# Attention of a float32 encoder layer: probabilities and values as whole float32 operands instead of split float16 halves, with the maxima chain reordered

## The chip, the core and the metric

One core of a Trainium2 chip runs the whole layer. The metric is device time in microseconds (us) of one execution, as the median of several. TensorE's clock is granted at one of two levels, 1.2 or 2.4 GHz; the profile gives it as 0.5 or 1.0 of full speed.

## What is computed

A one-layer encoder runs over two sequences, a prompt of 512 tokens and a sample of 2048 tokens, with model width 1024. Inputs, weights and outputs are float32. The layer normalises, projects, mixes with windowed means and with attention, projects back, and ends with a convolutional feed-forward part of width 2816. The change lies in the attention (8 heads, query and key width 96, value width 64):

```python
def attend(q_blk):
    s = jnp.einsum('bqhd,bkhd->bhqk', q_blk, k_full).astype(jnp.float32) * scale
    p = jax.nn.softmax(s, axis=-1).astype(v.dtype)
    return jnp.einsum('bhqk,bkhd->bqhd', p, v)
```

## The kernel before

The kernel has three stages. The first (to about 352 us) makes queries, keys and values in chunks of 256 tokens; queries and keys go through DRAM, values stay in SBUF in the tile `V`. The second (352 to about 1275 us) is the attention. The third (the rest) is the output projection and the feed-forward part.

To keep float32 accuracy with float16 products, an operand is *split*: a high half (the value rounded to float16) and a low half (what the rounding left). A product then needs three half-products, high by high, high by low and low by high (`THREE`); low by low is dropped. `V` holds per head 64 low columns, 64 high columns and a column of ones, so that one product with 129 moving columns gives low, high and the sum of the probabilities at once.

The attention runs in *units* in a hand-written order: 16 units of the prompt (256 queries by 4 key tiles of 128, two PSUM banks of scores) and 128 units of the sample (128 queries by 16 key tiles, four banks). The steps of a unit, by function:

- `st_scores`: a bank of scores, 12 products of 128 columns on TensorE (PE).
- `st_max`, `st_fold`: the maximum over a bank's four tiles on VectorE (DVE), one reduction for each of four banks into `mx4`, then the fold of the four maxima (128 x 512 elements) into `mx`.
- `st_T`, `st_redT`, `st_rep`: a transpose of `mx` on PE, its row maximum on DVE with two small operations that cut it into two parts (`p3`), a transpose back on PE, and a copy to `mr` on ScalarE (ACT).
- `st_r1`: four products that subtract the maximum from the score banks.
- `st_exp`: the exponential, one ACT operation a bank, into `pf` (float32).
- `st_hi`, `st_lo`: `pf` split into `ph` (one bank by ACT, the other three by DVE casts) and `pl` (GpSimd, POOL, four subtractions).
- `st_pv`: for each key tile a product of `ph` with 129 columns of `V` and one of `pl` with 65.
- `st_out`, `st_out2`: a copy of the result out of PSUM, the sum of the two halves (POOL), the division by the sum of probabilities (DVE), and a store once in four units.

The order is a string of letters, one turn of it for each unit `i`; each letter emits a step, and every engine runs its instructions in that order:

```python
r=lambda i: some(st_r1, i, range(4)),
L=lambda i: some(st_scores, i + 1, [3]),
a=lambda i: some(st_scores, i + 2, [0]),
M=lambda i: some(st_max, i + 1, [3]),
N=lambda i: run(st_fold, i + 1),
LAG = 2
PARTS = [0, 10, 16]
ORDER = "r e0 A L M N P o e1 a T d f l1 b R i c h l0 l2 l3 x y z q"
```

`A` and `P` are the two parts of `st_pv` of unit `i - LAG`, `b` and `c` score banks 1 and 2 of unit `i + 2`, `x y z` the maxima of banks 0 to 2 of that unit, `T d R` the transpose, row maximum and transpose back of unit `i + 1`. Score banks rotate through seven PSUM banks, so `L` needs the bank that the first exponential of the same turn frees, `a` that of the second, `b` and `c` the next two. One further PSUM bank (`psX`) holds the results of `st_pv` and the two transposes. Between turns, `prep_w_out` prepares the output weights, one small piece at a time; one piece is a POOL reduction over all partitions whose result DVE reads in the next piece.

Of the kernel before, what the change touches and what calls it, by code (L numbers as in the profile page):

```python
# [38 lines left out]
LN_SHIFT = math.log(2.0 ** 14)  # L39
SCORE_SCALE = 1.0 / math.sqrt(QKD)  # L40
VW = 130
# [7 lines left out]
def encoder(ctx, tc, ins, outs, seq_names=("x_prompt", "x_sample")):  # L49
# [27 lines left out]
    ln_shift = small([P, 1], "ln_shift")  # L77
    dve.memset(ln_shift, LN_SHIFT)
    act.activation(small([P, 1], "warm"), ln_shift, AF.Square)
# [103 lines left out]
    V = vpool.tile([P, NTOK // P, H, VW], F16, name="V")  # L183
    pool.memset(V[:, :, :, 128:130], 1.0)

# [28 lines left out]
    with tp("wA", 1) as wA, tp("pA", 2) as pA, tc.manual_schedule():  # L214
# [605 lines left out]
    def prep_w_out(raw):  # L820
# [20 lines left out]
        yield  # L841
# [51 lines left out]
    with tp("pB", 2) as pB, tp("psX", 1, "right", space=PSUM) as psX, \  # L893
# [49 lines left out]
        def st_max(i, b):  # L943
            u = units[i]
            w = u["w"]
            t0, t1 = u["banks"][b]
            st = u["st"][b]
            if t1 - t0 == 4:
                if b == 0:
                    u["mx4"] = pB.tile([P, 4, P], F32, name=f"mx4_{i}", tag="mx4")  # L950
                dve.tensor_reduce(u["mx4"][:, b, :], st.rearrange("p (t q) -> p q t", q=w), axis=AX.X, op=ALU.max)  # L951
            elif b:
                for t in range(2):
                    dve.tensor_tensor(out=u["mx"][:, :w], in0=st[:, t * w:(t + 1) * w], in1=u["mx"][:, :w], op=ALU.max)
            else:
                u["mx"] = pB.tile([P, 256], F32, name=f"mx_{i}", tag="mx")
                dve.tensor_reduce(u["mx"][:, :w], st[:, :(t1 - t0) * w].rearrange("p (t q) -> p q t", q=w), axis=AX.X,
                                  op=ALU.max)

        def st_fold(i):  # L960

            u = units[i]
            if len(u["banks"]) == 4:
                u["mx"] = pB.tile([P, 256], F32, name=f"mx_{i}", tag="mx")
                dve.tensor_reduce(u["mx"][:, 0:P], u["mx4"].rearrange("p b q -> p q b"), axis=AX.X, op=ALU.max)

        def side_tile(i):

            if ("x", i) not in state:
                state["x", i] = psX.tile([P, 512], F32, name=f"x_{i}", tag="x")  # L970
            return state["x", i]

        def st_T(i):
            u = units[i]
            xp = side_tile(i - 1)
            old = units[i - 1 - LAG]["nq"] if i > LAG else 1
            u["alone"] = u["nq"] > 1 or old > 1
            u["mrp"] = xp[:, 512 - u["w"]:] if u["alone"] else xp[:, 129:129 + P]
            xp = u["xp"] = xp[:, 512 - u["w"]:]
            for j in range(u["nq"]):  # L980
                pe.matmul(xp[:, j * P:(j + 1) * P], u["mx"][:, j * P:(j + 1) * P], ident, is_transpose=True,
                          start=u["alone"], stop=True, skip_group_check=True)

        def st_redT(i):
# [4 lines left out]
            dve.tensor_reduce(m, u["xp"][:, :nq * P].rearrange("p (j k) -> p j k", j=nq), axis=AX.X, op=ALU.max)  # L989
# [8 lines left out]
        def st_rep(i):  # L998
# [3 lines left out]
            for j in range(nq):  # L1002
                pe.matmul(u["mrp"][:, j * P:(j + 1) * P], p3[:, j].rearrange("p a b -> p (a b)"), ident,  # L1003
                          is_transpose=True, start=u["alone"], stop=True, skip_group_check=True)
# [18 lines left out]
        def st_exp(i, b):  # L1023
            u = units[i]
            if b == 0:
                u["pf"] = pB.tile([P, 2048], F32, name=f"pf_{i}", tag="pf")
# [4 lines left out]
        def st_hi(i, b):  # L1031
            u = units[i]
            if "ph" not in u:
                u["ph"] = pB.tile([P, 2048], F16, name=f"ph_{i}", tag="ph", bufs=3)
                u["pl"] = pB.tile([P, 2048], F16, name=f"pl_{i}", tag="pl", bufs=3)
            c = cols(u, b)
            if b == 2 and len(u["banks"]) == 4:
                c = slice(c.start, cols(u, 3).stop)
            if b in (1, 2):
                dve.tensor_copy(u["ph"][:, c], u["pf"][:, c])  # L1040
            elif b == 0:
                act.activation(u["ph"][:, c], u["pf"][:, c], AF.Copy)

        def st_lo(i, b):
            u = units[i]
            c = cols(u, b)
            pool.tensor_tensor(out=u["pl"][:, c], in0=u["pf"][:, c], in1=u["ph"][:, c], op=ALU.subtract)  # L1047

        def st_pv(i, part):
            u = units[i]  # L1050
            s, h, nq, nkt, w = u["s"], u["h"], u["nq"], u["nkt"], u["w"]
            if part == 0:
                op = side_tile(i + LAG) if units[min(i + LAG + 1, NU - 1)]["nq"] == 1 else bank(f"op_{i}")
                u["op"] = op[:, :2 * 129].rearrange("p (j c) -> p j c", j=2)
# [4 lines left out]
            parts = PARTS  # L1059
            for j, t in jobs[parts[part] * n // 16:parts[part + 1] * n // 16]:  # L1060
                c0 = t * w + j * P
                pe.matmul(op[:, j, 0:129], u["ph"][:, c0:c0 + P], V[:, k0 + t, h, 0:129], start=t == 0, stop=False)  # L1062
                pe.matmul(op[:, j, 64:129], u["pl"][:, c0:c0 + P], V[:, k0 + t, h, 64:129], start=False,  # L1063
                          stop=t == nkt - 1)

        def st_out(i):
# [7 lines left out]
            tt = state[key]  # L1074
            act.activation(tt[:, qi % 4:qi % 4 + nq, 0:129], op[:, 0:nq, 0:129], AF.Copy)  # L1075
            if (qi + nq) % 4 == 0 or (qi + nq) * P == s["S"]:
                n = qi % 4 + nq
                pool.tensor_tensor(out=tt[:, :n, 64:128], in0=tt[:, :n, 64:128], in1=tt[:, :n, 0:64], op=ALU.add)

        def st_out2(i):  # L1080
# [6 lines left out]
            if (qi + nq) % 4 == 0 or (qi + nq) * P == s["S"]:  # L1087
                n = qi % 4 + nq
                ri = pB.tile([P, 4], F32, name=f"ri_{i}", tag="ri")
                dve.reciprocal(ri[:, :n], tt[:, :n, 128])  # L1090
# [5 lines left out]
                dve.tensor_tensor(out=ot[:, :n, b0:b0 + 64], in0=tt[:, :n, 64:128],  # L1096
# [8 lines left out]
        LAG = 2  # L1105
        PARTS = [0, 10, 16]
# [12 lines left out]
        def some(fn, k, bs):  # L1119
            if 0 <= k < NU:  # L1120
                for b in bs:
# [6 lines left out]
            e0=lambda i: some(st_exp, i, range(3)),  # L1128
            e1=lambda i: some(st_exp, i, [3]),
            A=lambda i: run(st_pv, i - LAG, 0),  # L1130
            P=lambda i: run(st_pv, i - LAG, 1),
            
# [6 lines left out]
            v=lambda i: some(st_max, i + 3, [0]),  # L1139
            w=lambda i: some(st_max, i + 3, [1]),  # L1140
# [4 lines left out]
            N=lambda i: run(st_fold, i + 1),  # L1145
            f=lambda i: some(st_hi, i, [1]),
            h=lambda i: some(st_hi, i, [0]),
            i=lambda i: some(st_hi, i, [2]),
            l0=lambda i: some(st_lo, i, [0]),
            l1=lambda i: some(st_lo, i, [1]),  # L1150
            l2=lambda i: some(st_lo, i, [2]),
            l3=lambda i: some(st_lo, i, [3]),
# [5 lines left out]
        START = ["a b x y", "a b T d t x u y R", "r e T d t R x y u f l1 h l0",  # L1158
                 "r e T d t R x y u f l1 h l0", "r e T d A P R x y f l1 h l0 o q"]
        ORDER2 = "r e T d a b x R f l1 y h A P q o l0 c z"  # L1160
        ORDER = "r e0 A L M N P o e1 a T d f l1 b R i c h l0 l2 l3 x y z q"
        for i in range(-2, NU):
            whole = units[min(max(i, 0) + 1, NU - 1)]["nq"] == 1
            for x in (START[i + 2] if i + 2 < len(START) else ORDER if whole else ORDER2).split():
# [9 lines left out]
        for i in range(NU, NU + LAG):  # L1174
            for part in range(2):
                run(st_pv, i - LAG, part)
            run(st_out2, i - LAG - 1)
            run(st_out, i - LAG)
            m = i - NU
            if m == 1:  # L1180
# [3 lines left out]
            if m == LAG - 1:  # L1184
# [3 lines left out]
            for t, m in todo[:4]:  # L1188
                c_mm2(t, m)
# [532 lines left out]
```

## Time and profile before

| | us |
|---|---|
| median of 3 runs (3246.03 to 3251.99) | 3248.72 |
| the profiled execution, its own time | 3256.74 |
| its span | 3254.9 |
| PE busy in the span | 3044.8 |
| DVE busy | 2161.2 |
| ACT busy | 1400.4 |
| POOL busy | 875.7 |

Busy time over the whole span says little here: the third stage is 60% of the span and has nothing to do with the change. Read the stage by itself, with the busy time of each engine in a stretch of it, then the waits in that stretch, then one unit instruction by instruction. A time line gives start and duration in us; where it merges several instructions into one line, the duration runs from the first start to the last end. The end of a product is modelled, so what a product costs PE is read from the distance between two starts.

### The profile page before, as it was taken

The numbers are of one execution on the slowest core, as the hardware profiler recorded it, in microseconds if no ns is written. First come the engines' busy times: TensorE is split into PE (matmuls) and PEld (weight loads), VectorE is DVE, ScalarE is ACT, GpSimd is POOL, SyncE is SP. The second block draws the span as 40 slices with busy tenths as digits, with TensorE's granted clock in tenths as the row PEclk, the third lists the DMA queues.
The fourth block names the chain that finished last, engine by engine and source line by source line (L and its number), as shares of the span: only waits on it lengthen the run. The fifth ranks groups of instructions, "written<-read, shape, count | busy, mean of one in ns | idle before, by whom it ended". The sixth has DMA issues, their size and how long they took to land. (4 is left out here: it accounts for less than half of the span.)

```text
span 3254.9 us, 59928 instructions
## 1 busy us (share of the span) xinstructions
PE 3044.8 (94%) x24601; PEld 1959.7 (60%) x24601; DVE 2161.2 (66%) x4783; ACT 1400.4 (43%) x2863; POOL 875.7 (27%) x825
## 2 busy tenths in 40 slices
PE   6999888888887888999999999999999999999998
PEld 4777577777776776444555555555545555555554
DVE  6677788788887887335777777734357666674333
ACT  4554556556565665223333333433333333333333
POOL 1211467777776775221000000000100000000000
PEclk9999899999998999999999999999999999999999
DMA  3333221201110102576111111311161111113112
GB/s 133 105 108 92 72 50 34 70 5 24 31 22 8 28 4 75 190 220 168 45 47 40 40 39 40 112 36 36 57 150 40 51 41 39 40 38 102 42 38 75
DMA packets 272061, 210.37 MB, mean 65 GB/s; under 512 B 48739, under 2 KB 247722, under 8 KB 271530
## 3 DMA queue, kind: packets, MB, share of 16 engines
q1 hardware_dynamic: 270012, 200.23, 21.1%
q0 software_dynamic: 1440, 5.24, 0.4%
q8 instruction: 193, 3.16, 0.4%
q10 hardware_dynamic: 334, 1.06, 0.1%
q14 instruction: 82, 0.67, 0.1%
HBM read 140.51 MB, written 55.38 MB: 60 GB/s over the span
## 5 line engine op out<-in xcount | busy, mean ns | idle before, releaser
L1288 PE MATMUL up<-h,ws 128*128 128x512 f16 (+1 forms) x6336 | 1146.6, 344 | 7.3 <-DMA h<-h_x_sample 5.9
L1288 PEld LDWEIGHTS <-ws 128*128 128x128 f16 x6336 | 619.9, 98 | 533.3 <-issue 6.1
L1047 POOL TENSOR_TENSOR pl<-pf,ph 128x512 f16<-128x512 f32 x544 | 660.6, 1242 | 239.9 <-DVE ph L1040 197.0
L1387 PE MATMUL dn<-G,wds 128*128 128x512 f16 (+1 forms) x3168 | 579.0, 344 | 0.0
L939 PE MATMUL st<-Q,K 96*128 96x128 f16 (+1 forms) x6336 | 469.4, 225 | 3.3 <-ACT pf L1028 2.1
L1387 PEld LDWEIGHTS <-wds 128*128 128x128 f16 x3168 | 310.0, 98 | 254.2
L939 PEld LDWEIGHTS <-K 96*128 96x128 f16 x6336 | 420.9, 102 | 14.7 <-issue 3.8
L1028 ACT ACTIVATE pf<-st,ln_shift,cs 128x512 f32<-128x512 f32 x544 | 392.7, 774 | 56.6 <-PE st L1015 47.0
L951 DVE TENSOR_REDUCE mx<-st 128x128 f32<-128x512 f32 x512 | 329.3, 684 | 70.3 <-PE st L939 69.5
L1293 ACT ACTIVATE c<-up,ctab 128x511 f32<-128x511 f32 (+3 forms) x264 | 182.1, 699 | 407.4 <-PE up L1288 401.0
L1294 DVE SCALAR_TENSOR_TENSOR c<-up,ctab,c 128x510 f32<-128x510 f32 (+3 forms) x264 | 173.5, 657 | 185.7 <-ACT c L1293 183.0
L1062 PE MATMUL x<-V,ph 128*128 128x129 f16 x2072 | 238.4, 232 | 0.4 <-ACT t L1075 0.4
L1063 PE MATMUL x<-V,pl 128*128 128x65 f16 x2072 | 228.9, 202 | 6.6 <-POOL pl L1047 6.6
L1062 PEld LDWEIGHTS <-ph 128*128 128x128 f16 x2176 | 211.3, 105 | 32.3 <-issue 32.2
L1063 PEld LDWEIGHTS <-pl 128*128 128x128 f16 x2176 | 207.2, 103 | 7.7 <-POOL pl L1047 7.3
L1394 DVE SCALAR_TENSOR_TENSOR yt<-dn,yscB,yt 128x512 f32<-128x512 f32 (+1 forms) x48 | 31.5, 660 | 227.5 <-ACT yt L1393 217.7
L1297 DVE SCALAR_TENSOR_TENSOR c<-up,ctab,c 128x511 f32<-128x511 f32 (+1 forms) x264 | 174.7, 662 | 9.3
L1006 ACT ACTIVATE mr<-x 128x128 fp32r<-128x128 f32 (+1 forms) x143 | 41.2, 288 | 276.0 <-PE x L1003 276.0
L130 ACT ACTIVATE ws<-wr,sF 128x1024 f16<-128x1024 f32 x88 | 96.2, 1138 | 147.0 <-DVE sF L1265 142.0
L1335 POOL PARTITION_ALL_REDUCE imrA<-imxA x2 | 0.7, 374 | 576.9 <-DVE imxA L1333 576.9
L1262 POOL PARTITION_ALL_REDUCE war<-wam x22 | 7.8, 356 | 527.0 <-DVE wam L1260 520.6
L1415 POOL TENSOR_TENSOR y<-y,fng 128x512 f32<-128x512 f32 (+1 forms) x42 | 45.3, 1083 | 384.4 <-ACT yp L1406 349.7
(410 smaller groups left out, 3716.4 us busy)
## 6 DMA issues: line engine op xcount, KB each, us to landing
wr<-in_w_up SPq DMA_DIRECT2D x88, 512.0 KB, 4.9
wd<-in_w_down SPq DMA_DIRECT2D x32, 512.0 KB, 4.3
x_s<-in_x_sample SPq DMA_DIRECT2D x8, 1024.0 KB
xt_Cs<-in_x_sample SPq DMA_DIRECT2D x8, 1024.0 KB, 7.8
x_x_sample<-xt_Cs SPq DMA_DIRECT2D x8, 1024.0 KB, 4.0
h_x_sample<-rows_Cs SPq DMA_DIRECT2D x16, 512.0 KB, 2.7
wd<-in_w_down SPq DMA_DIRECT2D x16, 384.0 KB, 3.5
y<-x_x_sample SPq DMA_DIRECT2D x3, 2048.0 KB, 8.7
```

What stands on the lines that cost most here:

```text
L130: act.activation(hi, src, AF.Identity, scale=scale)
L939: pe.matmul(st[:, (t - t0) * w:(t - t0 + 1) * w], kt[:, x, t * P:(t + 1) * P], qt[:, y, u["q0"]:u["q0"] + w], start=n == 0 and t == t0, st ...
L951: dve.tensor_reduce(u["mx4"][:, b, :], st.rearrange("p (t q) -> p q t", q=w), axis=AX.X, op=ALU.max)
L1028: act.activation(u["pf"][:, c], u["st"][b][:, :c.stop - c.start], AF.Exp, bias=ln_shift[:, 0:1], scale=cs[:, 0:1])
L1047: pool.tensor_tensor(out=u["pl"][:, c], in0=u["pf"][:, c], in1=u["ph"][:, c], op=ALU.subtract)
L1062: pe.matmul(op[:, j, 0:129], u["ph"][:, c0:c0 + P], V[:, k0 + t, h, 0:129], start=t == 0, stop=False)
L1063: pe.matmul(op[:, j, 64:129], u["pl"][:, c0:c0 + P], V[:, k0 + t, h, 64:129], start=False, stop=t == nkt - 1)
L1288: pe.matmul(ps[:, :ncol], ws[side][:, k, x, :], ht[:, k, y, :ncol], start=m == 0, stop=m == 3 * KT - 1)
L1293: act.activation(c[:, :n], ps[:, :n], AF.Identity, scale=cw[:, 1, col:col + 1], bias=ctab[:, 3, col:col + 1])
L1294: dve.scalar_tensor_tensor(out=c[:, 1:n], in0=ps[:, 0:n - 1], scalar=cw[:, 0, col:col + 1], in1=c[:, 1:n], op0=ALU.mult, op1=ALU.add)
L1297: dve.scalar_tensor_tensor(out=c[:, 0:j1], in0=ps[:, 1:1 + j1], scalar=cw[:, 2, col:col + 1], in1=c[:, 0:j1], op0=ALU.mult, op1=ALU.add)
L1387: pe.matmul(acc[part][:, :n], w[f // 8][:, f % 8, x, :], G_[0][:, f, y, o:o + n], start=f in (0, NF - 1) and (x, y) == (0, 0), stop=f >= N ...
```

## The change

`V` becomes float32 with 64 columns of values and the column of ones; its low half is no longer made. The probabilities stay as `pf` (three buffers in place of two); `st_hi` and `st_lo` are gone, and so are the sum of the two halves and the bias of the exponential (a factor of 2^14). `st_pv` issues one float32 product of 65 columns for each key tile. `LAG` becomes 1, and `st_pv` comes in three parts (8, 5 and 3 of 16 tiles). The fold of the maxima covers three banks and is emitted at the end of the turn before (`F`); the fourth bank's maximum goes to its own tile `mx2`, is transposed beside `mx`, and the row maximum is taken over both (256 elements). The division moves from DVE to POOL. `prep_w_out` gets three more turns between the POOL reduction and its reader.

```diff
-VW = 130
+VW = 66
@@
-    V = vpool.tile([P, NTOK // P, H, VW], F16, name="V")
+    V = vpool.tile([P, NTOK // P, H, VW], F32, name="V")
@@
-                split(vt[:, :, 64:128], vt[:, :, 0:64], vps.rearrange("p (h d) -> p h d", h=H), pow2(-18))
+                act.activation(vt[:, :, 0:64], vps.rearrange("p (h d) -> p h d", h=H), AF.Copy, scale=pow2(-18))
@@
-        yield
+        for _ in range(4):
+            yield
         swo, swo_i = pow2_scale(amr2, 15)
@@
-                dve.tensor_reduce(u["mx"][:, 0:P], u["mx4"].rearrange("p b q -> p q b"), axis=AX.X, op=ALU.max)
+                dve.tensor_reduce(u["mx"][:, 0:P], u["mx3"], axis=AX.X, op=ALU.max)
@@
+            parts = [u["mx"][:, j * P:(j + 1) * P] for j in range(u["nq"])]
+            if u["nq"] == 1:
+                parts.append(u["mx2"])
...
-            dve.tensor_reduce(m, u["xp"][:, :nq * P].rearrange("p (j k) -> p j k", j=nq), axis=AX.X, op=ALU.max)
+            dve.tensor_reduce(m, u["xp"].rearrange("p (j k) -> p j k", j=nq), axis=AX.X, op=ALU.max)
@@
-            act.activation(u["pf"][:, c], u["st"][b][:, :c.stop - c.start], AF.Exp, bias=ln_shift[:, 0:1],
-                           scale=cs[:, 0:1])
...
-                dve.tensor_copy(u["ph"][:, c], u["pf"][:, c])
...
-            pool.tensor_tensor(out=u["pl"][:, c], in0=u["pf"][:, c], in1=u["ph"][:, c], op=ALU.subtract)
+            act.activation(u["pf"][:, c], u["st"][b][:, :c.stop - c.start], AF.Exp, scale=cs[:, 0:1])
@@
-                pe.matmul(op[:, j, 0:129], u["ph"][:, c0:c0 + P], V[:, k0 + t, h, 0:129], start=t == 0, stop=False)
-                pe.matmul(op[:, j, 64:129], u["pl"][:, c0:c0 + P], V[:, k0 + t, h, 64:129], start=False,
-                          stop=t == nkt - 1)
+                pe.matmul(op[:, j, :], u["pf"][:, c0:c0 + P], V[:, k0 + t, h, 0:65],
+                          start=t + j == 0 if u["apart"] else opens(i + LAG), stop=t == nkt - 1, skip_group_check=True)
@@
-                dve.tensor_tensor(out=ot[:, :n, b0:b0 + 64], in0=tt[:, :n, 64:128],
+                pool.tensor_tensor(out=ot[:, :n, b0:b0 + 64], in0=tt[:, :n, 0:64],
@@
-        LAG = 2
-        PARTS = [0, 10, 16]
+        LAG = 1
+        PARTS = [0, 8, 13, 16]
@@
-        ORDER = "r e0 A L M N P o e1 a T d f l1 b R i c h l0 l2 l3 x y z q"
+        ORDER = "r e A L a M x T d B b R y C o c z F q"
```

What stands in a row on DVE for one turn in the sample, before. `mx4_62` are the bank maxima of unit 62, `mx` the fold, `mc` the row maximum, `p3` its two parts, `ph` the casts.

```order
L951 TENSOR_REDUCE mx4_61_10687<-st_61_3_10720 128x128
L965 TENSOR_REDUCE mx_61_10734<-mx4_61_10687 128x128
L989 TENSOR_REDUCE mc_61_10764<-x_60_10699 128x1
L992 TENSOR_SCALAR p3_4274<-mc_61_10764 128x4
L995 TENSOR_SCALAR p3_4274<-mc_61_10764,p3_4274 128x4
L1040 CAST ph_60_10768<-pf_60_10695 128x512
L1040 CAST ph_60_10768<-pf_60_10695 128x1024
L951 TENSOR_REDUCE mx4_62_10806<-st_62_0_10750 128x128
L951 TENSOR_REDUCE mx4_62_10806<-st_62_1_10772 128x128
L951 TENSOR_REDUCE mx4_62_10806<-st_62_2_10789 128x128
```

The same turn on DVE, now. `mx2_61` is the maximum of the fourth bank.

```order
L966 TENSOR_REDUCE mx_61_9469<-mx3_61_9421 128x128
L951 TENSOR_REDUCE mx2_61_9515<-st_61_3_9489 128x128
L951 TENSOR_REDUCE mx3_62_9517<-st_62_0_9502 128x128
L998 TENSOR_REDUCE mc_61_9521<-x_60_9480 128x1
L1001 TENSOR_SCALAR p3_4252<-mc_61_9521 128x4
L1004 TENSOR_SCALAR p3_4252<-mc_61_9521,p3_4252 128x4
L951 TENSOR_REDUCE mx3_62_9517<-st_62_1_9530 128x128
L951 TENSOR_REDUCE mx3_62_9517<-st_62_2_9551 128x128
```

The fold now stands ahead of the last bank's maximum instead of behind it, one bank's maximum stands between that and the row maximum, and the casts are gone.

What stands on PE at the start of a turn, before: the subtraction of the maximum (`mr2`), then pairs of weight load and product for the high and the low half (`x` is the result in PSUM).

```order
L1015 MATMUL st_60_2_10547<-mr2_60_10667,ones2_4272 128x512
L1015 MATMUL st_60_3_10601<-mr2_60_10667,ones2_4272 128x512
L1062 LDWEIGHTS ph_58_10526
L1062 MATMUL x_60_10699<-V_90,ph_58_10526 128x129
L1063 LDWEIGHTS pl_58_10527
L1063 MATMUL x_60_10699<-V_90,pl_58_10527 128x65
```

The same place now, and then the place of the transposes.

```order
L1024 MATMUL st_60_2_9359<-mr2_60_9448,ones2_4250 128x512
L1024 MATMUL st_60_3_9393<-mr2_60_9448,ones2_4250 128x512
L1053 MATMUL x_60_9480<-V_88,pf_59_9379 128x65 x8
L937 LDWEIGHTS K_512_2_6560
```

```order
L990 MATMUL x_60_9480<-ident_60,mx_61_9469 128x128
L990 MATMUL x_60_9480<-ident_60,mx2_61_9515 128x128
L1053 MATMUL x_60_9480<-V_88,pf_59_9379 128x65 x5
```

A float32 product loads its weights itself, so no separate load is issued for it; the result comes from the unit just before (59 in turn 60) instead of the one before that, and part of it now stands behind the two transposes.

## Rows read from the trace of the kernel before

**Rows 1.** Busy us (x instructions) in stretches: PE, PEld, DVE, ACT, POOL, clock, DMA, GB/s.

```profile
650.00:1000.00 350.00, 299.76 (x4629) 260.90 (x4629) 297.22 (x601) 207.42 (x377) 267.83 (x227) 0.96 0.09 19
1400.00:3254.00 1854.00, 1832.53 (x10124) 993.35 (x10121) 1115.39 (x2554) 644.48 (x1386) 95.14 (x107) 1.00 0.23 66
```

**Rows 2.** Waits from 650 to 1250 us: total, times, longest.

```profile
PE x L981 <- DVE mx L965: 66.6, 87, 1.6
```

**Rows 3.** PE time line: start, us, what, idle before; one sample unit and the outermost ones.

```profile
429.14 0.30 PE L981 MATMUL x<-ident,mx 128*128 128x128 f32 x1 [1.03 <-DVE mx L965]
...
808.58 0.30 PE L981 MATMUL x<-ident,mx 128*128 128x128 f32 x1 [0.45 <-ACT pf L1028]
808.72 0.83 PE L939 MATMUL st<-Q,K 96*128 96x128 f16 x12
809.74 0.33 PE L1003 MATMUL x<-ident,p 128*128 128x128 f32 x1 [0.19 <-DVE p L995]
...
810.67 0.50 PE L1015 MATMUL st<-mr,ones 2*128 2x512 f32 x4
811.10 0.23 PE L1062 MATMUL x<-V,ph 128*128 128x129 f16 x1
...
811.90 0.22 PE L1062 MATMUL x<-V,ph 128*128 128x129 f16 x1
...
812.10 0.83 PE L939 MATMUL st<-Q,K 96*128 96x128 f16 x12
...
814.89 0.30 PE L981 MATMUL x<-ident,mx 128*128 128x128 f32 x1 [0.77 <-DVE mx L965]
...
1266.32 0.30 PE L981 MATMUL x<-ident,mx 128*128 128x128 f32 x1 [1.29 <-DVE mx L965]
```

**Rows 4.** DVE time line of the same unit.

```profile
808.92 0.29 DVE L989 TENSOR_REDUCE mc<-x 128x1 f32<-128x128 f32 x1 [0.49 <-PE x L981]
809.59 1.02 DVE L1040 CAST ph<-pf 128x512 f16<-128x512 f32 x2
810.53 1.88 DVE L951 TENSOR_REDUCE mx<-st 128x128 f32<-128x512 f32 x3
812.96 0.69 DVE L951 TENSOR_REDUCE mx<-st 128x128 f32<-128x512 f32 x1
813.69 1.06 DVE L965 TENSOR_REDUCE mx<-mx 128x128 f32<-128x512 f32 x1
```

**Rows 5.** ACT time line of the same unit.

```profile
811.27 2.12 ACT L1028 ACTIVATE pf<-st,ln_shift,cs 128x512 f32<-128x512 f32 x3 [0.36 <-PE st L1015]
```

**Rows 6.** PE groups by shape over the whole span: count, busy us, mean ns.

```profile
L279 PE MATMUL tp_s<-ident,x_s 128*128 128x128 f32 x128 | 19.1, 273 | 2.1 <-issue 2.1
L637 PE MATMUL mps_s<-pls_s,w_pl_s 128*128 128x256 f16 x96 | 11.8, 273 | 0.0
L981 PEld LDWEIGHTS x<-ident,mx 128*128 128x128 f32 x158 | 21.2, 143 | 122.7 <-ACT pf L1028 111.0 <-PE st L1015 6.8 <-issue 4.9
```

**Rows 7.** Time lines of PE and its weight loads: float32 transposes in a row.

```profile
335.34 0.27 PE L527 MATMUL tl_s<-ident,krr_s 128*32 128x128 f32 x1
335.45 0.27 PE L526 MATMUL tl_s<-ident,latn_s 128*128 128x128 f32 x1
...
335.34 0.14 PEld L526 LDWEIGHTS tl_s<-ident,latn_s 128*128 128x128 f32 x1
335.45 0.10 PEld L527 LDWEIGHTS tl_s<-ident,krr_s 128*32 128x32 f32 x1
```

**Rows 8.** The stall near 1010 us: PE and ACT time lines.

```profile
1001.79 0.30 PE L981 MATMUL x<-ident,mx 128*128 128x128 f32 x1 [0.76 <-DVE mx L965]
...
1017.72 0.42 PE L981 MATMUL x<-ident,mx 128*128 128x128 f32 x1
...
1013.40 2.12 ACT L1028 ACTIVATE pf<-st,ln_shift,cs 128x512 f32<-128x512 f32 x3 [9.29 <-POOL pl L1047]
```

**Rows 9.** Prompt units, 356 to 426 us: the row maximum over 256 elements, DVE group.

```profile
L989 DVE TENSOR_REDUCE mc<-x 128x2 f32<-128x256 f32 x15 | 6.3, 421 | 9.6 <-PE x L981 9.6
```

More of the change, by code (lines that the diff above doesn't have):

```diff
@@ L970, in side_tile, with opens @@
                 state["x", i] = psX.tile([P, 512], F32, name=f"x_{i}", tag="x")
+                state["new", i] = True
             return state["x", i]
+        def opens(i):
+            return state.pop(("new", i), False)
         def st_T(i):
             u = units[i]
[L975 to L982, printed above, removed]
+            x = side_tile(i - 1)
+            parts = [u["mx"][:, j * P:(j + 1) * P] for j in range(u["nq"])]
+            if u["nq"] == 1:
+                parts.append(u["mx2"])
+                u["xp"], u["mrp"] = x[:, 128:384], x[:, 384:512]
+            else:
+                u["xp"], u["mrp"] = x[:, 0:256], x[:, 256:512]
+            for j, part in enumerate(parts):
+                pe.matmul(u["xp"][:, j * P:(j + 1) * P], part, ident, is_transpose=True, start=opens(i - 1), stop=True,
+                          skip_group_check=True)
         def st_redT(i):
@@ L1025, in st_exp @@
             if b == 0:
-                u["pf"] = pB.tile([P, 2048], F32, name=f"pf_{i}", tag="pf")
+                u["pf"] = pB.tile([P, 2048], F32, name=f"pf_{i}", tag="pf", bufs=3)
             c = cols(u, b)
-            act.activation(u["pf"][:, c], u["st"][b][:, :c.stop - c.start], AF.Exp, bias=ln_shift[:, 0:1],
-                           scale=cs[:, 0:1])
[L1031 to L1039, printed above, removed]
-                dve.tensor_copy(u["ph"][:, c], u["pf"][:, c])
[L1041 to L1046, printed above, removed]
-            pool.tensor_tensor(out=u["pl"][:, c], in0=u["pf"][:, c], in1=u["ph"][:, c], op=ALU.subtract)
+            act.activation(u["pf"][:, c], u["st"][b][:, :c.stop - c.start], AF.Exp, scale=cs[:, 0:1])
         def st_pv(i, part):
@@ L1052, in st_pv @@
             if part == 0:
-                op = side_tile(i + LAG) if units[min(i + LAG + 1, NU - 1)]["nq"] == 1 else bank(f"op_{i}")
-                u["op"] = op[:, :2 * 129].rearrange("p (j c) -> p j c", j=2)
+                u["apart"] = nq > 1 or units[min(i + LAG + 1, NU - 1)]["nq"] > 1
+                op = bank(f"op_{i}") if u["apart"] else side_tile(i + LAG)
+                u["op"] = op[:, :nq * 65].rearrange("p (j c) -> p j c", j=nq)
             op = u["op"]
@@ L1073, in st_out @@
                 state[key] = pB.tile([P, 4, VW], F32, name=f"t_{i}", tag="tacc")
[L1074 to L1078, printed above, removed]
+            act.activation(state[key][:, qi % 4:qi % 4 + nq, 0:65], op, AF.Copy)
         def st_out2(i):
@@ L1157, in encoder @@
             q=lambda i: run(st_out2, i - LAG - 1))
-        START = ["a b x y", "a b T d t x u y R", "r e T d t R x y u f l1 h l0",
-                 "r e T d t R x y u f l1 h l0", "r e T d A P R x y f l1 h l0 o q"]
-        ORDER2 = "r e T d a b x R f l1 y h A P q o l0 c z"
-        ORDER = "r e0 A L M N P o e1 a T d f l1 b R i c h l0 l2 l3 x y z q"
+        START = ["a b x y", "a b T d t x u y R", "r e T d t R x y u", "r e T d t R x y u A B C o",
+                 "r e T d A B C R x y o q"]
+        ORDER2 = "r e T d a b x R y A B C o q c z F"
+        TURN = "r e A L a M x T d B b C o R y c z F q"
+        ORDER = "r e A L a M x T d B b R y C o c z F q"
         for i in range(-2, NU):
-            whole = units[min(max(i, 0) + 1, NU - 1)]["nq"] == 1
-            for x in (START[i + 2] if i + 2 < len(START) else ORDER if whole else ORDER2).split():
+            now, then = (units[min(max(k, 0), NU - 1)]["nq"] for k in (i, i + 1))
+            order = START[i + 2] if i + 2 < len(START) else ORDER if now == 1 else TURN if then == 1 else ORDER2
+            for x in order.split():
                 step[x](i)
@@ L1173, in encoder @@
         todo = [(0, 0), (0, 1), (1, 0), (1, 1), (0, 2), (1, 2), (0, 3), (1, 3)]
[L1174 to L1180, printed above, removed]
+        for m in range(2):
+            if m == 0:
+                for part in range(3):
+                    st_pv(NU - 1, part)
+                st_out(NU - 1)
+            else:
                 for mp in range(2):
@@ L1187, in encoder @@
                 list(split_w_out(x))
-            for t, m in todo[:4]:
-                c_mm2(t, m)
+            for t, k in todo[:4]:
+                c_mm2(t, k)
             del todo[:4]
```

38 lines of the change are left out of this document (13 added, 25 removed).

## The prediction

> **What bounds the kernel now.** I read the busy time by stretches first. In the attention no engine is full: from 650 to 1000 us PE is busy 299.8 of 350 us and DVE 297.2 [rows 1]. So an engine's total decides nothing there; the loop from unit to unit does. The wait table names the link: PE waits for the fold of the maxima 87 times, 66.6 us in all [rows 2]. The time line shows one turn: from transpose to transpose 6.31 us (808.58 to 814.89), with 0.77 us of PE idle before the second one [rows 3], while DVE does the fourth bank's maximum (0.69) and then the fold (1.06) [rows 4].
>
> What PE itself needs in a turn, from distances between starts [rows 3]: 0.43 for the subtraction of the maximum (810.67 to 811.10); four score banks (twelve products take 0.83 to the last modelled end, less the 0.23 of one product 0.60 for eleven starts, so 0.66 for twelve) 2.64; a transpose 0.14 (808.58 to 808.72), the transpose back counted alike; and 16 pairs of high and low product. Nine pairs lie between 811.10 and 811.90, so a pair costs 0.089, sixteen 1.42. Together 4.77 of 6.31: 1.5 us of a turn is waiting.
>
> From the first to the last sample transpose 837.2 us pass (429.14 to 1266.32) [rows 3]. At 6.31 the 128 units would take 807.7. Of the 29.5 above that, 9.6 are one stall: 15.9 us from 1001.79 to 1017.72, where ACT waited 9.3 us for POOL [rows 8]. The other 19.9 go mostly with the clock, 0.96 on average here and 1.00 in the third stage, where PE has hardly a gap [rows 1].
>
> **The change: the float32 product.** Its price is the term that decides, and the trace of before has no such product. A pair streams 129 + 65 = 194 columns in 0.089 us, 0.46 ns a column, and its float16 weight loads don't show. The split product is three half-products (low by high, high by high with the ones, high by low); an exact one of 65 columns has a fourth, low by low, so I count 4 x 65 = 260 columns: 0.119 us. Lower end: a float32 transpose of 128 columns lasts 273 ns, as does a float16 product of 256 [rows 6]; if two columns' time were all, 130 columns would cost 0.060. Upper end: nothing of the loads is hidden, with one load of 143 ns [rows 6] for each half of the weights: 0.119 + 0.286 = 0.405. I take 0.119, since in the nearest rows the load hides: float32 transposes start 0.11 us apart whether the load beside them takes 0.14 or 0.10 [rows 7].
>
> The Trainium skill, FP8 and Floating Point Precision, TensorE Precision Notes, says that true FP32 makes four passes through the array; no row here shows it. Against the change speaks the Trainium skill, TensorE: Matmul & The Clock Gate, on the fast weight load (not for FP32) and on LDWEIGHTS (columns / 1.2 in ns): as an estimate 107 ns for 128 columns, 213 ns for two loads, more than the stream of 0.119 us could hide, and a sum near 3,340 us. The trace disagrees in part: 96 columns more cost a load 0.04 us [rows 7], half of what that rule gives.
>
> **The change: one turn in the sample, walked through.** PE needs 0.43 + 2.64 + 0.25 (two transposes, the second at the 0.11 of [rows 7]) + 0.14 = 3.46, and 16 x 0.119 = 1.90: 5.36. The waits follow from the latencies of before [rows 3 to 5], counted from the subtraction at 0:
> - `A` (8 tiles) ends at 1.38. `L` needs the first exponential's bank: 1.43, as before (810.67 to 812.10). It ends at 2.09; `a` follows with the next exponential (2.12 / 3 = 0.71 later), 2.14 to 2.80.
> - `M` starts 0.86 after `L` (812.10 to 812.96): 2.29 to 2.98. No fold follows. The transpose comes 0.14 after DVE ends (814.75 to 814.89): 3.12. PE waits 0.2 there, in place of 0.77.
> - DVE has the next bank's maximum first (1.88 / 3, 0.6), then the row maximum at 3.60. To the transpose back it was 0.82 (808.92 to 809.74); the reduction over 256 instead of 128 elements adds 0.42 - 0.29 [rows 4, 9]: 4.55. `B` and `b` keep PE busy from 3.26 to 4.52, so the wait is 0.03.
> - `C` and `c` end at 5.71. The copy to `mr` is done by then (at most 0.93 after the transpose back, 809.74 to 810.67). The next turn starts: 5.71.
>
> The same walk over the order of before comes to 6.20 where the rows show 6.31, so I add 0.11: 5.82. Saved: 0.49 x 128 = **63 us**. Below 0.119 the product gives little (at 0.060 the exponential, `M` and DVE hold the turn at 5.5); above it, each 0.01 costs nearly 0.16 a turn.
>
> **The other parts.** The stall: POOL has no subtractions left to be late with, and the reader of the reduction comes three pieces later; **-10**. The clock: PE waits 0.3 a turn instead of 1.5; I take half of the 19.9, **-10** (0 to -20). The 16 prompt units lose one cast each on DVE, of 512 of the 1536 elements that take 1.02 in the sample [rows 4], 0.34 x 16 = 5.4, and the division: **-5** (0 to -10).
>
> Nothing, with the cover: the casts (1.02 a turn on DVE [rows 4]) stood behind the row maximum; their going is in the walk. The fold runs at the turn's end under the next subtraction and `A`; uncovered it would cost its 1.06 again. The smaller lag needs the previous unit's exponentials, which end near 3.6 of a turn of 5.8. The PSUM bank that `A` opens is freed by the copy after `C`, under `c` and the subtraction; the copy queues behind `mr` on ACT, and only the next `A` waits for it. The division on POOL delays stores that are read after the attention. The missing low halves of `V` free DVE in a stage where other work remains. At the end one `st_pv` fewer is pending, but the last waits for its own exponentials: 0, within 2 either way.
>
> Sum: -63 - 10 - 10 - 5 = -88. The profiled execution took 3256.7, so 3169; it stood 8.0 above the median, so **3160 us** against a median of 3248.7 (0.973). With the terms' own bounds 3125 to 3185.
>
> **Rivals.** *The weight loads show.* If each of the two float32 loads adds the 0.04 by which 128 columns exceed 32 [rows 7], a product costs 0.199. PE then needs 3.46 + 3.18, with 0.25 of waits and the 0.11 a turn of 7.00: +0.69 x 128 = 88, less the other 25: 3312, slower. For it speaks that float32 loads are longer and twice as many per column streamed; against it that the transposes hide theirs. It decides from 0.168 a product on, where the turn reaches 6.51 and eats the other gains. With nothing hidden (0.405) the turn is 10.3 and the time near 3,735. The skill's rule on loads, above, is this rival, and has the same chance.
>
> *Half of that shows.* One load in two sticks out, 0.159 a product: the turn is 3.46 + 2.54 + 0.3 + 0.11 = 6.41, +13 - 25 = -12: 3237.
>
> *DVE takes the place of the fold.* PE stands 0.03 from waiting at the transpose back. If the row maximum from PSUM or the queue on DVE comes 0.35 later than in the walk, PE waits that long in each turn: 45 us of the 88 go, 3205. For it: the maximum of the next bank now stands ahead of the row maximum, on purpose a longer way. Against it: DVE has 1.02 of casts less.
>
> **How the numbers follow.** Forecast 0.58 (3125 to 3185). Loads show 0.21 (3262 and up). Half shows 0.13 (3190 to 3255). DVE 0.08 (3180 to 3215). The range takes in all but the first rival: 3120 to 3262. A measurement here can tell about 0.2%, 6.5 us, from no change. Faster by more than that: 0.58 + 0.08 + 0.09 of the half = 0.75; within it the upper part of the half, 0.04; slower 0.21.
>
> **What would show it.** Right: from transpose to transpose 5.7 to 5.9 at full clock; float32 products about 0.12 apart between `A`'s first and last; PE's wait before the transposes of the maxima near 0.2; no gap of 9 us near 1010; the clock in the attention above 0.96. Wrong: products 0.17 or more apart (first rival), products at 0.12 but PE idle before the transpose back (third), or a turn near 5.8 with more half-clock stretches than before.

## The result: 33% slower, and the profile after

The changed kernel takes **4325.81 us** (4310.88 to 4332.22) against 3249.14 (3246.03 to 3251.99) for the kernel before: a ratio of 1.331 (95% interval 1.327 to 1.335). The prediction was 3160, with 3120 to 3262 as its range. The profiled execution took 4330.37 us, span 4328.6, at a mean granted clock of 0.776 where the kernel before had 0.978.

The page of the changed kernel: busy time of two engines, then two rows over 40 equal slices of the span (108 us each; tenths busy, and the granted clock in tenths of 2.4 GHz), then the PE group of the product of probabilities and values (line 1053; in later rows line 937 is the scores, 990 the transposes of the maxima, 1012 the transpose back, 1024 the subtraction).

```profile
PE 4119.2 (95%) x24729; PEld 2960.3 (68%) x24729; DVE 1969.7 (46%) x4450; ACT 1269.1 (29%) x2719; POOL 212.7 (5%) x281
PE   7999999999999999999999999999999999999998
PEclk9997555555555555555556999999999999999999
L1053 PE MATMUL x<-V,pf 128*128 128x65 f32 x4096 | 962.3, 419 | 140.6 <-DVE mc L998 86.5
```

The clock row is the news: from the fifth slice to the twenty-first, which is nearly the whole of the sample's attention, the granted clock is 0.5: PE ran at 1.2 instead of 2.4 GHz. PE is at the same time 9 or more tenths busy in each of these slices, so the busy row shows nothing of it. And there are 4096 records of the product where 128 units of 16 key tiles make 2048: one float32 product is **two** records, each with a weight load of its own.

Stretches of the changed kernel (columns as in [rows 1]); the first answers to the first of [rows 1].

```profile
650.00:1000.00 350.00, 323.71 (x2028) 293.09 (x2029) 94.96 (x194) 67.53 (x139) 3.06 (x5) 0.51 0.10 24
2400.00:4300.00 1900.00, 1886.08 (x10355) 1014.82 (x10354) 1131.70 (x2572) 653.79 (x1392) 110.44 (x115) 1.00 0.23 69
```

In the same 350 us PE completes 2028 instructions instead of 4629; clock 0.51 instead of 0.96; DVE falls from 297 us to 95, POOL from 268 to 3. Behind the attention the clock is 1.00 as before, and that stage has not changed: nearly all of the 1077 us between the two medians lie in the attention.

One turn, the PE time line (start, us, line, count, idle before), to be set beside [rows 3]:

```profile
807.68 3.67 PE L1053 MATMUL x<-V,pf 128*128 128x65 f32 x16
811.15 2.76 PE L937 MATMUL st<-Q,K 96*128 96x128 f16 x24
813.71 0.63 PE L990 MATMUL x<-ident,mx 128*128 128x128 f32 x2
815.03 2.40 PE L1053 MATMUL x<-V,pf 128*128 128x65 f32 x10 [0.69 <-DVE mc L998]
817.22 1.48 PE L937 MATMUL st<-Q,K 96*128 96x128 f16 x12
818.50 0.42 PE L1012 MATMUL x<-ident,p 128*128 128x128 f32 x1
819.35 1.54 PE L1053 MATMUL x<-V,pf 128*128 128x65 f32 x6 [0.43 <-ACT mr L1015]
...
828.85 0.63 PE L990 MATMUL x<-ident,mx 128*128 128x128 f32 x2
```

The turn is 15.14 us (813.71 to 828.85) where the prediction had 5.82. Read by distances between starts: `A`, the first eight products, takes 3.47 for 16 records, 0.217 each; twelve scores take 1.28 instead of 0.66. The wait for the fold of the maxima is gone, as predicted, and so is the stall near 1010 us: ACT waits for POOL nowhere in the sample's attention. But two idle stretches stand where the walk had none: `B`, 0.69 us, until DVE has read the row maximum out of tile `x`, and `C`, 0.43 us, until ACT has copied `mr` out of it. `x` is the PSUM bank into which the products themselves go, so a product behind a transpose waits for the reader of that transpose.

That the shared bank makes the wait, the same trace shows by itself. In the turn of the first sample unit the products are still those of the last prompt unit (`LAG` is 1), and they go to a bank of their own (`op`). Here are that turn and the next, from their transposes on, both at the low clock:

```profile
441.78 0.64 PE L990 MATMUL x<-ident,mx 128*128 128x128 f32 x2
442.20 0.95 PE L1053 MATMUL op<-V,pf 128*128 128x65 f32 x4
...
453.89 0.63 PE L990 MATMUL x<-ident,mx 128*128 128x128 f32 x2
455.21 2.40 PE L1053 MATMUL x<-V,pf 128*128 128x65 f32 x10 [0.69 <-DVE mc L998]
```

With `op` the product starts 0.42 us behind the transposes, with `x` 1.32 us.

### The profile page after: what moved, and what is told of

Same layout as the page of the kernel before. It is cut to its first block, busy times and chain, and to the rows that moved or that the text cites. A ratio compares the mean times of both kernels' runs of the same rounds, so it can differ in the third digit from the quotient of the medians.

```text
span 4328.6 us, 58943 instructions
## 1 busy us (share of the span) xinstructions
PE 4119.2 (95%) x24729; PEld 2960.3 (68%) x24729; DVE 1969.7 (46%) x4450; ACT 1269.1 (29%) x2719; POOL 212.7 (5%) x281
## 3 DMA queue, kind: packets, MB, share of 16 engines
q10 hardware_dynamic: 334, 1.06, 0.1%
## 5 line engine op out<-in xcount | busy, mean ns | idle before, releaser
L1053 PE MATMUL x<-V,pf 128*128 128x65 f32 x4096 | 962.3, 419 | 140.6 <-DVE mc L998 86.5
L1053 PEld LDWEIGHTS x<-V,pf 128*128 128x128 f32 x4096 | 891.2, 326 | 282.4 <-DVE mc L998 137.0
L937 PE MATMUL st<-Q,K 96*128 96x128 f16 (+1 forms) x6336 | 754.2, 309 | 0.7 <-ACT t L1064 0.7
L937 PEld LDWEIGHTS <-K 96*128 96x128 f16 x6336 | 722.7, 151 | 6.7 <-issue 1.4
L1037 ACT ACTIVATE pf<-st,cs 128x512 f32<-128x512 f32 x544 | 330.2, 688 | 227.3 <-PE st L1024 226.3
L132 DVE SCALAR_TENSOR_TENSOR wds<-wd,fs,wds 128x128 f16<-128x128 f32 x352 | 114.1, 381 | 51.5 <-ACT wds L127 51.5
L132 DVE SCALAR_TENSOR_TENSOR ws<-wr,sF,ws 128x1024 f16<-128x1024 f32 x88 | 109.2, 1280 | 26.3 <-ACT ws L127 26.3
L127 ACT ACTIVATE wds<-wd,fs 128x128 f16<-128x128 f32 x352 | 107.7, 387 | 35.6 <-DVE fs L1343 31.7
L127 ACT ACTIVATE G<-c,p2s 128x511 f16<-128x511 f32 x132 | 76.4, 641 | 140.4 <-DVE invG L1291 109.7
L1024 PE MATMUL st<-mr,ones 2*128 2x512 f32 x544 | 111.6, 777 | 1.0 <-ACT mr L1015 1.0
```

What stands on the lines that cost most here:

```text
L127: act.activation(hi, src, AF.Identity, scale=scale)
L132: dve.scalar_tensor_tensor(out=lo, in0=src, scalar=scale, in1=hi, op0=ALU.mult, op1=ALU.subtract)
L937: pe.matmul(st[:, (t - t0) * w:(t - t0 + 1) * w], kt[:, x, t * P:(t + 1) * P], qt[:, y, u["q0"]:u["q0"] + w], start=n == 0 and t == t0, st ...
L1024: pe.matmul(u["st"][b][:, :n * w].rearrange("p (t q) -> p t q", q=w), ones2[r, :], u["mr"][r, :w].rearrange("p (o q) -> p o q", o=1).to_br ...
L1053: pe.matmul(op[:, j, :], u["pf"][:, c0:c0 + P], V[:, k0 + t, h, 0:65], start=t + j == 0 if u["apart"] else opens(i + LAG), stop=t == nkt - ...
```

## The experiments

Three things had to be told apart: the price of a float32 product, the two waits, and the clock. Each of the ten kernels changes one or two of them. The two with the chain alone ran ten times each, the last one four times; the other seven ran once, so their times are single executions. Letters are those of the kernel's own orders: `r` subtraction of the maximum, `e` exponentials, `A B C` parts of the product, `L a b c` score banks, `M x y z` their maxima, `F` the fold, `T` transposes of the maxima, `d` the row maximum, `R` the transpose back.

### The product alone, in the order of before

```
-  pe.matmul(op[:, j, 0:129], u["ph"][..], V[.., 0:129], ..)
-  pe.matmul(op[:, j, 64:129], u["pl"][..], V[.., 64:129], ..)
+  pe.matmul(op[:, j, 0:65], u["pf"][..], V[.., 0:65], ..)      # pf, V float32; the halves are still made
```

> The order, the lag of 2, the maxima chain and all work of the kernel before, the probabilities still split on ACT, DVE and POOL; only the values are float32 and the product is one float32 product for each key tile, reading the unsplit probabilities. Theory A (the float32 product itself brings the clock down): attention at a clock of 0.5, a turn near 15 us, total near 4300 us. Theory B (the new order and the shorter lag bring it down, the product costs only its 0.22 us at full clock): clock 0.9 or more, PE work a turn 3.35 + 16 x 0.22 = 6.9, with a waits' share of 1 a turn of 7.9, total near 3450 us.

Measured 3411.21 us, clock 0.988. One turn on PE, from transpose to transpose:

```profile
806.34 0.30 PE L981 MATMUL x<-ident,mx 128*128 128x128 f32 x1
...
807.50 0.33 PE L1003 MATMUL x<-ident,p 128*128 128x128 f32 x1 [0.18 <-DVE p L995]
...
808.87 2.45 PE L1062 MATMUL x<-V,pf 128*128 128x65 f32 x20
811.15 0.83 PE L939 MATMUL st<-Q,K 96*128 96x128 f16 x12
811.82 1.50 PE L1062 MATMUL x<-V,pf 128*128 128x65 f32 x12
...
813.96 0.30 PE L981 MATMUL x<-ident,mx 128*128 128x128 f32 x1
```

The turn is 7.62. Twenty records take 2.28 us (808.87 to 811.15): 0.114 each at full clock, 0.228 a product. PE is the bound, with 0.18 us of idle time left; the fold and its wait no longer matter. So float32 products do not bring the clock down in this order, but they cost 5% even at full clock. The clock came out as the second expectation had it, the turn 0.3 us below it.

### What a product's price depends on

The same kernel, with each product done as two narrow ones:

```
-  pe.matmul(op[:, j, 0:65], u["pf"][..], V[.., 0:65], ..)
+  pe.matmul(op[:, j, 0:33], u["pf"][..], V[.., 0:33], ..)
+  pe.matmul(op[:, j, 33:65], u["pf"][..], V[.., 33:65], ..)
```

> The run with the product alone, each float32 product of 65 columns replaced by two, of 33 and of 32 columns, with the same result. Theory L (each float32 product is two loads and two streams, one after the other, the loads 0.057 us each and not hidden): 0.168 a narrow product, 0.336 a key tile instead of 0.223, a turn of 7.62 + 1.8 = 9.4 us, total near 3650 us. Theory S (only the columns cost, the loads are hidden): the two cost what the one did, a turn of 7.6 to 7.8 us, total 3410 to 3440 us.

Measured 4711.22 us, clock 0.789. Both levels of the clock stand within one turn here. The time line at the low one (the first two rows) and at the full one (the last two); each row is one product, two records:

```profile
798.40 0.62 PE L1062 MATMUL x<-V,pf 128*128 128x33 f32 x2
...
801.39 0.61 PE L1064 MATMUL x<-V,pf 128*128 128x32 f32 x2
...
812.75 0.39 PE L1064 MATMUL x<-V,pf 128*128 128x32 f32 x2
...
813.87 0.39 PE L1062 MATMUL x<-V,pf 128*128 128x33 f32 x2
```

Seven products from 798.40 to 801.39: 0.427 each; five from 812.75 to 813.87: 0.224. At full clock a product of 32 columns costs what one of 65 costs. Both expectations were wrong: between 32 and 65, columns don't enter the price; it is that of two records, each with its weight load. By the Trainium skill, TensorE: Matmul & The Clock Gate, on LDWEIGHTS, two loads of 128 columns come to 213 ns, an estimate; the trace agrees within 7% at full clock (0.226 with 65 columns), and at the low one a product took twice that (0.427). That the load is what sets a record's price fits this and is not shown apart: float32 transposes stand 0.11 us apart too, beside a load of 128 columns or of 32 [rows 7]. The stretch of 350 us that the first of [rows 1] covers:

```profile
650.00:1000.00 350.00, 350.00 (x2391) 340.26 (x2391) 107.37 (x212) 76.94 (x142) 97.19 (x80) 0.59 0.06 16
```

PE never waits here and its loads are busy nearly throughout, and the mean granted clock is 0.59. A PE that the profile shows as full can stand at 1.2 GHz.

### The chain of maxima alone, halves kept

```
-ORDER = "r e0 A L M N P o e1 a T d f l1 b R i c h l0 l2 l3 x y z q"
+ORDER = "r e0 A L M N P o e1 a T d f l1 b R i c h l0 l2 l3 x y z F q"   # F: fold of three banks; N: join with the fourth
```

The join of the fourth bank's maximum is an elementwise maximum of two operands in the first kernel, a reduction over pairs in the second.

> The kernel before with only the maxima chain rebuilt: the fold covers three banks at the end of the turn before, the fourth bank's maximum is joined to it by one operation over 128 x 128 elements; split halves, lag 2 and the order else are kept. Theory A: no float32 product, so the clock stays at 0.95 or above; the transpose waits for the joining (about 0.25 us) instead of the fold (1.06), a turn of 5.6 to 5.8 instead of 6.31, total 3160 to 3190 us. Theory B: the rebuilt chain brings the clock down, turns above 8 us, total above 3450 us.

> The run with the chain alone, but the fourth bank's maximum is joined by a reduction over 256 elements instead of the two-operand maximum, which took 0.32, 0.52 and 0.91 us in three turns while POOL was running. Theory C (the two-operand operation on DVE is slowed by POOL, a reduction is not): the join takes 0.4 us in every turn, a turn of 5.6 to 5.8 us, total 3160 to 3190 us. Rival (DVE's total, 5.5 us a turn with the casts, or POOL's 5.0 holds the turn): a turn of 6.2 or more, total 3230 to 3255 us.

Measured 3251.86 us, ratio 1.0008 (0.9993 to 1.0023), and 3245.36, ratio 0.9988 (0.9974 to 1.0003): no change, against the first expectation of either kernel. The reason stands in DVE's groups from 460 to 960 us (busy us, mean ns): fold and join by a reduction, then the elementwise join of the other kernel:

```profile
L966 DVE TENSOR_REDUCE mx<-mx 128x128 f32<-128x384 f32 x77 | 42.6, 553 | 2.7
L973 DVE TENSOR_REDUCE mx<-mx 128x128 f32<-128x256 f32 x77 | 32.4, 420 | 2.6
```

```profile
L974 DVE TENSOR_TENSOR mx<-mx,mx 128x128 f32<-128x128 f32 x77 | 36.8, 478 | 2.6
```

Fold and join by reductions come to 0.97 us, the old fold to 1.06 [rows 4]; the elementwise join takes 478 ns on average, 0.29 while POOL is idle and up to 0.91 while it works. With the reduction, what DVE does between the fourth bank's scores and the transpose falls from 1.75 us (0.69 + 1.06) to 1.11 (0.69 + 0.42), and the turn does not. DVE is busy 428.5 of these 500 us and waits for scores 18.8 (35.5 before), and PE still waits 39.6 for the join (56.7 for the fold before): by these numbers DVE's row as a whole, with the fold at its end and the casts, now holds the turn, as the rival of the second kernel had it. What the new chain gives once the casts are gone, no run shows apart.

### The changed kernel without its float32 product

```
+ pw = u["pf"].bitcast(bfloat16)[:, 2 * c0 + 1:2 * (c0 + P):2]     # upper 16 bits, likewise of V
```

The products use the upper 16 bits of probabilities and values: the rest is left out. Once in the changed kernel's order, once with all three parts together ahead of the transposes:

```
-ORDER = "r e A L a M x T d B b R y C o c z F q"
+ORDER = "r e A B C L a M x T d b R o y c z F q"
```

> The changed kernel with its order, lag and chain, but in the sample each key tile's product reads only the upper 16 bits of the probabilities and the values, as one bfloat16 product of 65 columns (lower accuracy; the prompt's products stay float32). Theory A: without the float32 product the clock is back at 0.95 or above, a turn of 5.5 to 5.8 us, total 3120 to 3180 us. Theory B: the clock stays near 0.5, PE work of 2 x (3.5 + 0.5) = 8 us, a turn near 8.7, total near 3550 us.

> The same order as the run with all products together, but the sample's products are bfloat16 ones of 65 columns on the upper 16 bits (lower accuracy). Theory W: with the waits gone the clock is 0.9 or above, a turn of 5.5 to 5.9 us, total 3130 to 3190 us. Rival (a turn with little PE work loses the clock whatever its order): PE has about 4 us of work in a turn, the clock falls to 0.5 for most of the attention, a turn above 8 us, total above 3450 us.

Measured 3591.55 us, clock 0.831, and **3083.66**, clock 0.994. Stretches of the two kernels, in this order, each with its turn:

```profile
650.00:1000.00 350.00, 299.90 (x2683) 251.90 (x2680) 159.06 (x330) 110.84 (x226) 5.53 (x9) 0.50 0.09 21
811.20 0.63 PE L990 MATMUL x<-ident,mx 128*128 128x128 f32 x2
812.51 0.43 PE L1057 MATMUL x<-V,pf 128*128 128x65 bf16 x5 [0.69 <-DVE mc L998]
...
820.48 0.63 PE L990 MATMUL x<-ident,mx 128*128 128x128 f32 x2
```

```profile
650.00:1000.00 350.00, 309.53 (x4693) 254.69 (x4694) 274.29 (x589) 188.59 (x403) 11.07 (x18) 1.00 0.12 26
801.92 0.61 PE L990 MATMUL x<-ident,mx 128*128 128x128 f32 x2
...
807.22 0.61 PE L990 MATMUL x<-ident,mx 128*128 128x128 f32 x2
```

The first has the two waits (0.69 and 0.42) and in the sample no float32 product; its clock is 0.50 through the sample's attention, its turn 9.28. The second computes the same with the waits gone: 1.00, and 5.29. So in these two runs the place of `B` and `C` made the difference between 1.2 and 2.4 GHz, without a float32 product.

### The float32 product in other orders

The same new order with the float32 product kept; then one with scores between the parts:

```
+ORDER = "r e A B C L a M x T d b R o y c z F q"     # together
+ORDER = "r e A L B a C M x T d b R o y c z F q"     # spread
```

> The changed kernel with only the place of the float32 products moved: all 16 of a turn stand before the scores, so none stands between a transpose and its reader in the PSUM bank that they share. Theory W (the waits of the products behind those readers, 0.69 and 0.43 us a turn at the trace of the changed kernel, make the gaps that bring the clock down): clock 0.95 or above in the attention, PE work 3.46 + 16 x 0.223 = 7.0, a turn of 7.4 to 7.7 us, total 3380 to 3430 us. Theory K (the shorter lag or another part of the new order does): clock 0.5, a turn of 14 us or more, total above 4200 us.

> The changed kernel in another order: all three parts of a unit's float32 products stand ahead of its transposes T, with 12 products of the scores between the parts, so that no part waits for the reader of the bank that it shares (0.69 us behind T and 0.43 us behind R in the changed kernel) and no row of products is longer than 16 records (32 in the run with the products together). Theory W (the granted clock was lost to those waits and to the long row): clock over 0.97, a turn near the 8.08 us that the run with the products together had while its clock was full, less what scores now cover, 7.6 to 8.1, and 3,410 to 3,470 us. Theory R (the records themselves do it, in whatever rows they stand): the clock falls to 0.5 at some point of the attention as with the products together, turns of 13 to 14 us there, 3,700 to 4,000 us.

Together: 3978.78 us, clock 0.828. Products and the scores behind them, from PE's time line:

```profile
570.62 3.79 PE L1053 MATMUL x<-V,pf 128*128 128x65 f32 x32
574.24 1.50 PE L937 MATMUL st<-Q,K 96*128 96x128 f16 x24
...
578.70 3.79 PE L1053 MATMUL x<-V,pf 128*128 128x65 f32 x32
...
691.86 5.77 PE L1053 MATMUL x<-V,pf 128*128 128x65 f32 x32
...
704.20 7.09 PE L1053 MATMUL x<-V,pf 128*128 128x65 f32 x32
711.08 2.76 PE L937 MATMUL st<-Q,K 96*128 96x128 f16 x24
...
717.85 7.09 PE L1053 MATMUL x<-V,pf 128*128 128x65 f32 x32
```

```profile
704.00:1954.00 1250.00, 1250.00 (x7958) 1167.09 (x7955) 386.65 (x800) 262.24 (x558) 14.85 (x24) 0.50 0.04 10
```

At the low clock PE waits for nothing in this order, the instructions are the same from turn to turn, and yet the turn goes from 8.08 us (570.62 to 578.70) to 13.65 (704.20 to 717.85), within the row at 691.86, and stays there to the end of the attention. Neither expectation foresaw both levels. 32 records take 3.62 us at the full clock and 6.88 at the low one: 0.226 and 0.430 a product. Spread: 3456.68 us, clock 0.973; one turn:

```profile
804.72 0.39 PE L990 MATMUL x<-ident,mx 128*128 128x128 f32 x2
...
807.47 2.00 PE L1053 MATMUL x<-V,pf 128*128 128x65 f32 x16
809.30 0.83 PE L937 MATMUL st<-Q,K 96*128 96x128 f16 x12
809.97 1.28 PE L1053 MATMUL x<-V,pf 128*128 128x65 f32 x10
...
812.43 0.39 PE L990 MATMUL x<-ident,mx 128*128 128x128 f32 x2
...
813.81 0.33 PE L1012 MATMUL x<-ident,p 128*128 128x128 f32 x1 [0.32 <-DVE p L1004]
```

This order too ran at either level: 0.54 from 435 to 578 us, with PE busy 142.7 of these 143 us, and then 0.98 to 1.00 to the end of the attention, at a turn of 7.71. Moving `B` and `C` ahead of the transposes, with scores between them, gives back 869 of the 1077 us in this run. The same work in a long row stands between the two.

### More work, less time

```
-for n, (x, y) in enumerate(THREE):
+for n, (x, y) in enumerate(((0, 0), (0, 1), (1, 0), (1, 1))):   # a fourth half-product of the scores
```

> The changed kernel with a fourth half-product (low by low) in every score: 16 float16 products of 128 columns more in each sample turn, nothing taken away. Theory A1 (float32 products hold the clock down whatever runs beside them): clock 0.5, a turn of 15.1 + 16 x 0.107 = 16.9 us, total near 4550 us. Theory A2 (what counts is how much float16 streaming stands beside them): the clock comes back, a turn of 7.5 + 0.9 = 8.4 us, total near 3500 us, faster than the changed kernel although PE does more.

The changed kernel with 16 more float16 products in a turn takes 3670.83 us, **655 less**, at clock 0.992.

```profile
805.82 0.39 PE L990 MATMUL x<-ident,mx 128*128 128x128 f32 x2
...
813.85 1.95 PE L937 MATMUL st<-Q,K 96*128 96x128 f16 x32
815.64 0.39 PE L990 MATMUL x<-ident,mx 128*128 128x128 f32 x2
816.91 1.33 PE L1053 MATMUL x<-V,pf 128*128 128x65 f32 x10 [0.89 <-DVE mc L998]
...
819.68 0.88 PE L1053 MATMUL x<-V,pf 128*128 128x65 f32 x6 [0.43 <-ACT mr L1015]
```

Both waits are there, the second as long, the first longer, and the float32 products too; only float16 work was added, and the clock stayed up. So neither the waits nor the float32 products decide the clock alone: with both, it stayed up here. The second expectation had the direction right and the turn too short (8.4). By what the added work brings the clock back, no run shows. The turn is 9.81; less 16 products of 0.056 (32 take 1.79, 813.85 to 815.64) it is 8.91, my estimate for the changed kernel's own turn at full clock.

### A version faster than both

Products together, probabilities written as float16 by the exponential (shifted by 2^14), values as float16: the low halves of both are left out, so this version computes with less accuracy.

```
+ u["pf"] = pB.tile([P, 2048], F16, ..)
+ act.activation(u["pf"][:, c], .., AF.Exp, bias=ln_shift[:, 0:1], scale=cs[:, 0:1])
```

> The changed kernel with the products together ahead of the transposes, and with probabilities (shifted by 2^14 in the exponential) and values written as one float16 half each instead of float32: the low halves of both are left out. If the price is that of the float32 records and the waits alone, this gives the turn of the bfloat16 run in the same order, 5.3 us, at a clock over 0.98: 3,080 to 3,090 us, some 5% below the kernel before. Rival: a float16 write of the exponential or a float16 weight load is dearer than the bfloat16 view of float32 (ScalarE 688 ns for each exponential now; a turn over 5.6 us): 3,120 us or more.

Measured **3099.81 us**, ratio 0.952 (0.949 to 0.954), clock 0.986, turn 5.38: 0.09 a turn more than with the upper 16 bits, and a time between the two that were expected. Exponentials of that kernel and of this one:

```profile
L1037 ACT ACTIVATE pf<-st,cs 128x512 f32<-128x512 f32 x379 | 229.8, 689 | 60.2 <-PE st L1024 60.2
```

```profile
L1039 ACT ACTIVATE pf<-st,ln_shift,cs 128x512 f16<-128x512 f32 x372 | 258.9, 776 | 59.0 <-PE st L1026 59.0
```

The exponential takes 776 ns instead of 689, and PE now waits 0.26 us for it in each turn. The kernel before had 774 with the same shift as a bias operand and a float32 output, so the 87 ns go with the bias and not with the output's type.

## Why the prediction was wrong, step by step

**What bounds the kernel before: half right.** PE does wait for the fold. But taking most of it off that path alone left the turn as it was, because DVE's row took its place; the prediction had ruled out an engine's total there. With the casts gone as well, a cheap product in place of the halves and no waits in `x`, the turn falls from 6.31 to 5.29.

**The product's price: mis-sized, and the choice of row with it.** It was put at 0.119 us; it is 0.226 at full clock. The two steps that failed: counting 4 x 65 columns, where columns don't enter the price (32 cost what 65 cost), and taking the float32 transposes of [rows 7] as a sign that the load hides. Their 0.11 us from start to start is what one float32 record takes, and a product is two records of 0.113. The rival that the loads show was nearest: it had 0.199 and, in its sentence on the Trainium skill, 213 ns. By the walk's own sum with 0.226 the turn is 3.46 + 3.62 + 0.25 + 0.11 = 7.44, and 7.62 and 7.71 were measured at full clock. So a right price would have forecast some 3370, slower, and still some 950 us short.

**The waits: missing from the walk.** The step that failed is where PE goes on behind the transposes. The walk followed DVE to the row maximum and asked when `R` could start, but let `B` start right behind the transposes and `C` right behind `R`. Both write the bank that DVE and ACT are then reading. In the order of before no product stood at these two places. Measured 0.69 and 0.43 us a turn; the estimate at full clock is 1.20 (8.91 against 7.71 with the parts moved).

**The clock: wrong in sign, and the bulk of the time.** The step said: less waiting, so a higher clock, -10 us. Measured is 0.51 instead of 0.96 between 650 and 1000 us. The step took busy time for what keeps the clock. The runs show PE without a gap at 0.50 (products together, from 704 to 1954 us) and 87% busy at 1.00 (four scores, 303.5 of 350 us).

Put together, a turn goes from 6.31 to 7.71 by the product (net of what the rest gains), to 8.91 by the waits, to 15.14 by the clock: +1.40, +1.20 and +6.23. The first of these is the turn of the order with the products spread, the second and third split at the estimate of 8.91. Times 128: 179, 154 and 797 us, 1130 in all. Between the first and the last transpose back of the sample the mean turn is 6.59 before (430.30 to 1267.48, with the stall) and 14.93 after (435.80 to 2331.73), which makes 127 x 8.34 = 1059 of the 1074 us between the two profiled spans.

**Two slips of the sums.** The walk lets `B` start behind one transpose and not behind two (3.26 for 3.37); put right, its turn is 5.79 and not 5.71, 10 us in all. And between the first and the last transpose of the sample there are 127 turns, not 128, which makes the 29.5 us above the plain turns 35.8. Neither changes the outcome.

**Right in kind:** the stall near 1010 us is gone, the wait for the fold is gone, the casts' and POOL's work is gone. **Not tested apart:** the prompt units and the end.

**What stays open.** Why the clock falls. The runs name cases, not a law, most of them from one execution: waits in `x` with bfloat16 products, 0.50; float32 products in a row of 32, either level; in rows of 20 and 12 in the order of before, 1.00; in rows of at most 16 with scores between, 0.54 for 143 us and then 1.00; with more float16 work, 1.00 in spite of the waits. What tipped the row of 32 near 694 us, with the same instructions on either side, no view here shows; whether another execution of the spread order would stay at 1.00, no run shows. Products in a bank of their own in the whole attention were not tried: in this kernel the other seven banks hold scores.

## What to carry to other kernels

Price a float32 product of few columns by its records, two of 0.113 us with a weight load each: at 32 to 65 columns it cost 0.226 us, where the pair of split float16 halves took 0.089. Before moving a product behind a transpose, ask who still reads the bank that it writes. And where a change trades float16 products for float32 ones, or puts waits among PE's products, price the stage at both clock levels: here it fell from 2.4 to 1.2 GHz, and that outweighed everything else in the sum.

## What the runs showed of the hardware

- A float32 product of 128 x 128 weights is two load-and-product records, 0.112 to 0.114 us each at 2.4 GHz and 0.213 to 0.217 at 1.2, with 32, 33 or 65 columns alike.
- Adding 16 float16 products to each turn made the kernel 655 us faster, with more work and no shorter waits: the granted clock went from 0.51 to 1.00 between 650 and 1000 us.
- The same instructions ran at 8.08 us a turn for a while and at 13.65 afterwards, at a granted clock of 1.00 and then of 0.50 (products together).
- PE stood at a granted clock of 0.50 for 1250 us without an idle stretch in the profile (products together, 704 to 1954 us).
- An exponential with a bias operand takes 774 ns for 128 x 512 into float32 and 776 into float16; without the bias it takes 688 to 689 into float32.
